# Norm weights on the sync queue, matmul order pinned between sublayers, and twelve weight units per feed-forward part in tiles of the attention

## The chip, the cores and the metric

The kernel runs on one core of a Trainium2 chip. The metric is the device time of one execution in microseconds (us). A profiled execution also has a span, from its first to its last instruction; the time is a little longer than the span.

## The reference

Four layers work on x of 256 rows and 1024 columns, in float32. Each layer is an attention sublayer and then a feed-forward sublayer, and each sublayer is wrapped in two norms:

```
for i in range(4):
    hn = rms_norm(x, norm_gains[i, 0])
    m  = mixer[i % 3](hn)             # a: differential attention, b: stick-breaking, c: sliding window with sinks
    x  = x + rms_norm(m, norm_gains[i, 1])
    f  = (silu(h @ w_gate) * (h @ w_up)) @ w_down,  h = rms_norm(x, norm_gains[i, 2])
    x  = x + rms_norm(f, norm_gains[i, 3])
```

The hidden width is 2816. Layers 0 and 3 use mixer a, layer 1 mixer b, layer 2 mixer c. Mixers a and c rotate queries and keys by position (rope).

## The kernel before

**Streams and units.** The 256 rows are two streams, s=0 and s=1, of 128 rows each. All weights are cut into 378 units of 128x1024 numbers. A unit is fetched by the sync queue (SP) into one of STAGE=4 tiles `stage`. ScalarE (ACT) then rounds it into `hi`, and VectorE (DVE) writes the remainder `lo` (function `split`, L254). Both live in a ring of RING=11 tiles each. Stream 0 uses a unit first, stream 1 some units later; the ring slot is free when stream 1 is done with it. With 512 columns a stream spends six matmuls of 512 columns on a unit: hi and lo by the rounded activations (`xh`), and hi by their remainder (`xl`), each twice.

**The order of emission.** `Emitter` (L42) is a planner that runs while the program is built. Each stream is a generator; it asks for a unit, waits for an event, or sleeps for some planned nanoseconds (`yield ("d", 4000)`). Shorter generators, its tasks, turn tiles and compute scores. The planner's clock `t` moves forward with every emitted matmul. Stream 0 goes first unless stream 1 is behind an edge (the start of an output projection, or the end of a layer). Stream 0 may lead by at most LAG=8 units, and units are split at most AHEAD=3 beyond stream 0 and RING=11 beyond stream 1:

```
while self.loaded < min((self.pos[0] + AHEAD if self.pos[0] else 2), free, self.limit):
...
return self.pos[s] in self.ring and (lag < (LAG if self.pos[1] > 3 else 3) if s == 0 else lag > 0)
```

**The order on the engines.** The framework's scheduler may reorder what was emitted: it fills each engine's list with the instruction of the best rank that its own model believes ready. The list is then fixed, and an engine works through it in order. An instruction wrapped in `tc.keep_in_program_order` comes behind everything emitted before it on its engine; later ones that are not wrapped may still be moved ahead of it. The class `Start` (L172) wraps the calls of an engine while its flag `on` is set. `act.on`, `dve.on` and `pool.on` are cleared in layer 0 when stream 1's first norm is emitted, `pe.on` after stream 1's first projected chunk (L516).

**Around the change.** Between two sublayers a stream runs `post_norm` (squares on ACT, `r` on GpSimd (POOL), `mg` and the new `x` on DVE), sleeps 4000, runs `pre_norm` (eight transposes `tp_q` or `tp_n` of `x` on TensorE (PE), `xh` on ACT, `xl` on DVE), sleeps 600 and asks for its first unit. In the feed-forward part, chunk c takes four units of gate and up weights, and from c=1 on two units of down weights (`down`, results `acc_f`) follow. The hidden values `h_f` go through POOL (`hp_f`), a transposing DMA and POOL again (`hx_f`) before ACT and DVE split them into `hTh_f` and `hTl_f`. In mixer c, task `keys` (L806) ropes the first chunk on DVE into `kd_c`, then transposes it on PE (`tk_c`). In mixer a, task `turned` (L604) ropes a chunk into `t_a...` on DVE and then transposes it (`tt_a...`).

**The start.** `rows`, the norm weights as 128x128, and `pos_i`, the positions, are fetched on ACT's queue in that order (L276, L278). On SP's queue come x of stream 0, two units, x of stream 1 and two more units. `tables()` (L317) works on DVE from the positions, and the copy `gains` of the turned norm weights follows it there; `xh_n` needs `gains`.

**Tiles of the attention.** Keys and values have a tile for each group g and stream s (`kT{g}{s}`, `V{g}{s}`), attention weights one for each stream (`wT{s}`). Once stream 1's attention output is turned, nothing reads them until the next layer.

Of the kernel before, what the change touches and what calls it, by code (L numbers as in the profile page):

```python
# [9 lines left out]
F32 = mybir.dt.float32  # L10
# [31 lines left out]
class Emitter:  # L42
# [3 lines left out]

    def __init__(self, load_dma, split, n_units, edges):
        self.t = 0.0  # L50
        self.load_dma, self.split, self.n, self.edges = load_dma, split, n_units, edges
        self.issued = self.loaded = 0
        self.pos = [0, 0]
        self.ring = {}
        self.events = set()
        self.limit = 0
        self.tasks = []
# [10 lines left out]
            self.issued += 1  # L68

    def advance(self):  # L70
        free = self.pos[1] + RING
        while self.loaded < min((self.pos[0] + AHEAD if self.pos[0] else 2), free, self.limit):
            self.fetch(self.loaded + STAGE)
            self.ring[self.loaded] = self.split(self.loaded)
            self.loaded += 1

    def run_task(self, task):
        while True:
# [34 lines left out]
    def can(self, m):  # L113
        if m["done"]:
            return False
        if m["want"] is None:
            return True
        if m["want"] == "w":
            s = m["s"]
            lag = self.pos[0] - self.pos[1]  # L120
            return self.pos[s] in self.ring and (lag < (LAG if self.pos[1] > 3 else 3) if s == 0 else lag > 0)
        return m["want"] in self.events

    def run(self, gens):
# [34 lines left out]
def trunk_kernel(ctx, tc, x, positions, norm_gains, a_w_in, a_w_out, a_lambda, a_subln, b_w_in, b_w_out,  # L159
# [12 lines left out]
    class Start:  # L172


        def __init__(self, engine):
            self.engine, self.on = engine, True
# [37 lines left out]
    def downs(c):  # L214

        return range(c - 1, c) if 0 < c < NCH - 2 else range(NCH - 3, NCH) if c == NCH - 1 else ()

    for i in range(depth):
        kind, inst = i % 3, i // 3
        if kind in (0, 1):  # L220
            w_in, w_out = (a_w_in[inst], a_w_out[inst]) if kind == 0 else (b_w_in[inst], b_w_out[inst])
            for g in range(2):
                for part in range(3):
                    chunk512(w_in, part * 1024 + 512 * g)
        else:
            w_in, w_out = c_w_in[inst], c_w_out[inst]
            chunk256(w_in, 1024)
            for g in range(4):
                chunk256(w_in, 256 * g)
        edges.append(len(units))  # L230
        for kt in range(KT):
            rows_unit(w_out, kt)
        for c in range(NCH):
            gate_up(i, c)
            for d in downs(c):
                for j in range(2):
                    rows_unit(w_down[i], 2 * d + j)
        edges.append(len(units))

    staged = {}  # L240
# [12 lines left out]

    def split(u):  # L254
        t = staged.pop(u)
        hi = ringp.tile([P, 1024], F32R, tag="hi", name=f"hi_{u}")
        lo = ringp.tile([P, 1024], F32R, tag="lo", name=f"lo_{u}")
        act.activation(hi, t, AF.Copy)
        dve.tensor_tensor(lo, t, hi.bitcast(F32), ALU.subtract)
        return hi, lo  # L260

    em = Emitter(load_dma, split, len(units), edges)


    zero = wk.tile([P, P], BF16, tag="t2k", name="zero", bufs=TMP)
# [7 lines left out]
    warming(WARM // 2)  # L273

    rows = wk.tile([P, P], F32, tag="t2k", name="rows", bufs=TMP)
    nc.scalar.dma_start(rows, norm_gains.rearrange("l n (k p) -> (l n k) p", p=P))  # L276
    pos_i = wk.tile([2, P], I32, tag="t2k", name="pos_i", bufs=TMP)
    nc.scalar.dma_start(pos_i, positions.rearrange("b (s p) -> (b s) p", p=P))  # L278
    xs = [cst.tile([P, D], F32, name=f"x_{s}") for s in range(2)]
# [222 lines left out]
    def project(s, xn, n, units_, name, first, tag="mm"):  # L502

        b = bank("acc" if first else tag, s, [P, n], f"mm_{name}")
        per = KT // units_
        for u in range(units_):
            w = yield ("w",)
            js = [(per * u + j, slice(j * n, (j + 1) * n)) for j in range(per)]
            pairs = [(kt, cs, v) for kt, cs in js for v in range(2)]
            if pe.on:  # L510
                pairs.sort(key=lambda x: x[2])
            for kt, cs, v in pairs:
                mm(b, xn[0][:, kt, :], w[v][:, cs], kt == 0 and v == 0, False)
            for kt, cs in js:
                mm(b, xn[1][:, kt, :], w[0][:, cs], False, kt == KT - 1)
        if s:  # L516
            pe.on = False
        return b

    def rope(b, n, cr, sr, name, outs=None):  # L520
# [28 lines left out]
        act.activation(dst, tp, AF.Copy)  # L549

    kT, V = {}, {}

    def queries(s, n, name):
        return wk.tile([P, n, P], F32, tag=f"qT{s}", name=f"qT_{name}", bufs=1)
# [41 lines left out]
    def layer_a(s, i, xn):  # L596
# [7 lines left out]
        def turned(chunk, g, which):  # L604
            t = rope(chunk, 8, *tabs[which], f"{name}{g}{which}")
            yield ("d", 2000)
            dst = None
            if which == "k":
                dst = kT[g, s] = wk.tile([P, 4, P], F32, tag=f"kT{g}{s}", name=f"kT_{name}{g}", bufs=1)
            else:  # L610
                dst = qT[g] = queries(s, 4, f"{name}{g}")
            four_transposes(s, t.rearrange("p h d -> p (h d)"), dst, f"tt_{name}{g}{which}")
            em.set((name, which, g))
            if which == "k":
                yield from scores(g)
# [73 lines left out]
        for g in range(2):  # L689
            for which in "qkv":  # L690
                chunk = yield from project(s, xn, 512, 4, f"{name}{g}{which}", g == 0 and which == "q")
                if not tabs:
                    tabs.update(scaled_tables(s, xn[2], name))
                if which == "v":
                    V[g, s] = wk.tile([P, 512], F32, tag=f"V{g}{s}", name=f"V_{name}{g}", bufs=1)
                    act.activation(V[g, s], chunk, AF.Copy, scale=xn[2])
                    em.set((name, "v", g))
                    em.spawn(values(g))
                    yield ("d", 600)
                else:  # L700
                    em.spawn(turned(chunk, g, which))
                    yield ("d", 1500)
        return oT, name

    def layer_b(s, i, xn):
# [6 lines left out]
        def turned(chunk, g, which):  # L712
            t = wk.tile([P, 512], F32, tag="t2k", name=f"t_{name}{g}{which}", bufs=TMP)
            act.activation(t, chunk, AF.Copy, scale=xn[2])
            yield ("d", 900)
            dst = None
            if which == "k":
                dst = kT[g, s] = wk.tile([P, 4, P], F32, tag=f"kT{g}{s}", name=f"kT_{name}{g}", bufs=1)
            else:
                dst = qT[g] = queries(s, 4, f"{name}{g}")  # L720
            four_transposes(s, t, dst, f"tt_{name}{g}{which}")
            em.set((name, which, g))
            if which == "k":
                yield from scores(g)
# [60 lines left out]
        for g in range(2):  # L785
            for which in "qkv":
                chunk = yield from project(s, xn, 512, 4, f"{name}{g}{which}", g == 0 and which == "q")
                if which == "v":
                    V[g, s] = wk.tile([P, 512], F32, tag=f"V{g}{s}", name=f"V_{name}{g}", bufs=1)
                    act.activation(V[g, s], chunk, AF.Copy, scale=xn[2])  # L790
                    em.set((name, "v", g))
                    em.spawn(values(g))
                    yield ("d", 600)
                else:
                    em.spawn(turned(chunk, g, which))
                    yield ("d", 600)
        return oT, name

    def layer_c(s, i, xn):
# [6 lines left out]
        def keys(chunk):  # L806
            kd = wk.tile([P, 2, 2, 64], F32, tag="t2k", name=f"kd_{name}", bufs=TMP)
            rope(chunk[:, 0:P], 2, *tabs["k"], f"{name}k", [kd[:, :, 0, :], kd[:, :, 1, :]])
            V["c", s] = wk.tile([P, P], F32, tag=f"V0{s}", name=f"V_{name}", bufs=1)
            act.activation(V["c", s], chunk[:, P:2 * P], AF.Copy, scale=xn[2])  # L810
            yield ("d", 1200)
            tp = bank("tp", s, [P, 2, P], f"tk_{name}")
            for c in range(2):
                transpose(tp[:, c, :], kd[:, c].rearrange("p a d -> p (a d)"))
            t = kT["c", s] = wk.tile([P, 2, P], F32, tag=f"kT0{s}", name=f"kT_{name}", bufs=1)
            act.activation(t, tp, AF.Copy)
            em.set((name, "k"))

# [117 lines left out]
    def stream(s):  # L936
        if s:
            yield ("d", 1500)
        for i in range(depth):
            kind = i % 3  # L940
            xn = pre_norm(s, 4 * i, f"n{i}{s}")
            yield ("d", 600)
            if i == 0 and s:
                em.spawn(scalars())
            oT, name = yield from (layer_a, layer_b, layer_c)[kind](s, i, xn)
            gain = gain_of(i, 1)
            acc = yield from out_proj(s, oT, name, (1, 1, 3)[kind])
            post_norm(s, acc, gain, f"m{i}{s}")
            yield ("d", 4000)
            gain = gain_of(i, 3)  # L950
            xn = pre_norm(s, 4 * i + 2, f"q{i}{s}")
            yield ("d", 600)
            acc = yield from ffn(s, i, xn)
            post_norm(s, acc, gain, f"e{i}{s}")
            if i < depth - 1:
                yield ("d", 4000)
        for h in range(2):
            cs = slice(h * 512, (h + 1) * 512)
# [28 lines left out]
```

## Time and profile before

| | |
|---|---|
| median of three runs | 1187.56 us (1186.59 to 1187.84) |
| profiled execution | 1186.93 us, span 1185.1 us |
| granted TensorE clock | 0.998 |
| busy: PE, DVE, ACT, POOL | 1162.8, 784.8, 654.4, 216.9 us |
| instructions | 16743 |

In timeline rows the columns are start, duration, engine, line, operation, out<-in, count, and in brackets the idle time of the engine before it with what ended it. Nearly all rows name L182, since the class `Start` issues most instructions from there; they are told apart by tile names. Rows that end in q (SPq, ACTq) are issues of DMAs. The end of a matmul is modelled, so losses on PE are best read from one start to the next.

### The profile page before, as it was taken

The page shows a single profiled execution, that of the slowest core. Times are in us where ns is not written, and L with a number is a line of the kernel's source. Part 1 is how long each engine was busy: PE and PEld are TensorE (multiplying, and loading weights), DVE is VectorE, ACT ScalarE, POOL GpSimd, SP SyncE. Part 2 cuts the span into 40 slices and gives each one's busy share as a digit, 9 for nine tenths or more (in the row PEclk, how much of TensorE's full clock was granted, in tenths as well). Part 3 has the DMA queues.
Part 4 walks back from the last instruction along what each step waited for, and adds up shares of the span by engine and source line. Part 5 has one row for each costly group of instructions (what it writes and reads, how often), then busy time and mean ns, then how long its engine had stood idle before and what let it go on. Part 6 is the DMA issues. An engine that isn't in the chain of part 4 may idle for free.

```text
span 1185.1 us, 16743 instructions
## 1 busy us (share of the span) xinstructions
PE 1162.8 (98%) x5869; PEld 954.8 (81%) x5869; DVE 784.8 (66%) x1226; ACT 654.4 (55%) x1209; POOL 216.9 (18%) x301
## 2 busy tenths in 40 slices
PE   8999999999999999999999999999999999999997
PEld 6787788888878878888888878888878788888886
DVE  7876666665847666666588666666686775766563
ACT  6665654444766655445476655444475565544441
POOL 2100133221200013222210013222210001322221
PEclk9999999999999999999999999999999999999999
DMA  7635468777643646777664346777765364687761
GB/s 265 208 126 177 129 195 231 202 220 207 216 128 125 213 129 196 206 217 212 203 195 154 108 129 196 215 212 216 207 195 155 130 192 150 178 211 213 209 194 40
DMA packets 183948, 216.41 MB, mean 183 GB/s; under 512 B 52788, under 2 KB 148152, under 8 KB 183864
## 3 DMA queue, kind: packets, MB, share of 16 engines
q1 hardware_dynamic: 183716, 215.28, 60.9%
q8 instruction: 46, 0.75, 0.2%
q14 instruction: 38, 0.31, 0.1%
q10 hardware_dynamic: 148, 0.07, 0.0%
HBM read 203.76 MB, written 1.05 MB: 173 GB/s over the span
## 4 chain that ended last, share of the span: by engine, by line
PE 90%; DVE 3%; ACT 2%; issue 2%; DMA 1%; POOL 1%; DVEq 0%; ACTq 0%; POOLq 0%; SPq 0%
PE mm_f L182 39%; PE acc_f L182 19%; PE acc_a L182 3%; PE mm_c L182 2%; PE acc_b L182 2%; PE sc_a L182 2%; PE acc_c L182 2%; DVE lo L182 1%; ACT hi L182 1%; PE sc_c L182 1%; PE sc_b L182 1%; DMA stage<-in_a_w_in_dram 1%; PE pv_a L182 1%; DVE x L182 1%; PE tp_q L182 1%
## 5 line engine op out<-in xcount | busy, mean ns | idle before, releaser
L182 DVE TENSOR_TENSOR lo<-stage,hi 128x1024 fp32r<-128x1024 f32 x378 | 459.5, 1225 | 160.0 <-ACT hi L182 157.8
L182 ACT ACTIVATE hi<-stage 128x1024 fp32r<-128x1024 f32 x378 | 395.1, 1057 | 166.2 <-PE mm_f L182 85.7
L182 PE MATMUL mm_f<-hi,xh_q 128*128 128x512 f32 x704 | 275.4, 391 | 1.5 <-ACT hi L182 1.5
L182 PE MATMUL mm_f<-lo,xh_q 128*128 128x512 f32 x704 | 274.0, 389 | 0.0
L182 PE MATMUL mm_f<-hi,xl_q 128*128 128x512 f32 x704 | 217.0, 389 | 0.4 <-DVE xl_q L182 0.4
L182 POOL COPY hp_f<-h_f 128x512 uint16<-128x512 uint16 x80 | 92.0, 1149 | 408.2 <-DVE h_f L182 408.2
L182 PEld LDWEIGHTS mm_f<-hi,xh_q 128*128 128x128 f32 x704 | 132.1, 188 | 30.3 <-ACT hi L182 3.2
L182 PEld LDWEIGHTS mm_f<-hi,xl_q 128*128 128x128 f32 x704 | 132.1, 188 | 28.9 <-DVE xl_q L182 1.3
L182 PEld LDWEIGHTS mm_f<-lo,xh_q 128*128 128x128 f32 x704 | 132.2, 188 | 27.0
L182 ACT ACTIVATE hTh_f<-hx_f 128x256 fp32r<-128x256 f32 x80 | 33.4, 418 | 163.4 <-POOL hx_f L182 163.4
L182 PE MATMUL acc_f<-hi,hTh_f 128*128 128x512 f32 x352 | 111.4, 392 | 1.2 <-ACT hTh_f L182 1.2
L182 PE MATMUL acc_f<-lo,hTh_f 128*128 128x512 f32 x352 | 109.8, 389 | 0.0
L182 PE MATMUL acc_f<-hi,hTl_f 128*128 128x512 f32 x352 | 109.8, 389 | 0.0
L182 DVE TENSOR_TENSOR hTl_f<-hx_f,hTh_f 128x256 fp32r<-128x256 f32 x80 | 33.8, 423 | 103.5 <-ACT hTh_f L182 103.5
L182 POOL COPY hx_f<-hq_f 128x512 uint16<-128x512 uint16 x80 | 80.5, 1006 | 84.1 <-DMA hq_f<-hp_f 83.8
L182 ACT ACTIVATE t_f<-mm_f,half_f 128x256 f32<-128x256 f32 x88 | 41.5, 472 | 77.4 <-PE mm_f L182 77.4
L182 PEld LDWEIGHTS acc_f<-hi,hTh_f 128*128 128x128 f32 x352 | 65.8, 188 | 15.5 <-ACT hTh_f L182 2.4
L182 PEld LDWEIGHTS acc_f<-lo,hTh_f 128*128 128x128 f32 x352 | 66.1, 188 | 13.8
L182 PEld LDWEIGHTS acc_f<-hi,hTl_f 128*128 128x128 f32 x352 | 66.0, 188 | 13.7
L182 DVE SCALAR_TENSOR_TENSOR t_f<-t_f,mm_f 128x256 f32<-128x256 f32 x88 | 36.7, 417 | 34.3 <-ACT t_f L182 34.3
L182 DVE SCALAR_TENSOR_TENSOR h_f<-t_f,hsq_f,mm_f 128x256 f32<-128x256 f32 x88 | 42.2, 480 | 2.9
L182 ACT ACTIVATE e_a<-sc_a,nm_a 128x128 f32<-128x128 f32 (+1 forms) x64 | 26.1, 421 | 16.5 <-DVE nm_a L182 16.4
(588 smaller groups left out, 1545.5 us busy)
## 6 DMA issues: line engine op xcount, KB each, us to landing
stage<-in_ffn_w_gate_dram SPq DMA_DIRECT2D x176, 256.0 KB, 3.0
stage<-in_ffn_w_up_dram SPq DMA_DIRECT2D x176, 256.0 KB, 3.2
stage<-in_ffn_w_down_dram SPq DMA_DIRECT2D x88, 512.0 KB, 4.4
stage<-in_a_w_in_dram SPq DMA_DIRECT2D x48, 512.0 KB, 4.2
stage<-in_b_w_in_dram SPq DMA_DIRECT2D x24, 512.0 KB, 4.1
stage<-in_a_w_out_dram SPq DMA_DIRECT2D x16, 512.0 KB, 3.7
stage<-in_c_w_in_dram SPq DMA_DIRECT2D x10, 512.0 KB, 4.0
gain<-in_norm_gains_dram SPq DMA_DIRECT2D x8, 512.0 KB, 5.1
```

What stands on the lines that cost most here:

```text
L182: i = call(*args, **kw)
```

## The change

1. `rows` is fetched first on SP's queue, ahead of x; `pos_i` is then alone on ACT's queue.
2. `hold` keeps a count that starts at 2. Every `post_norm` that another sublayer follows adds one, and every stream's first unit of a sublayer, after its matmuls, takes one away; `pe.on` is set while the count is above 0. So PE's instructions are pinned to the order of emission while a stream is between sublayers. At the start this ends after each stream's first unit, earlier than before. The sort of pairs in `project` now goes by `act.on`.
3. The sleep behind `pre_norm` is 1100 in place of 600, other than ahead of layer 0.
4. Each feed-forward part has 66 units. Twelve of them (k = 2, 5, 8, 16, 19, 22, 30, 33, 36, 44, 47, 50) are split into the tiles `kT0`/`V0`, `kT1`/`V1` or `wT1` in place of ring slots, once stream 1's attention output is turned (event `("a01", "o", 7)` and the like). `lead` lets stream 0 be ahead by LAG plus the number of such units from 11 behind it to 2 beyond, so by up to 11.
5. For this the two groups' keys share a tile for each stream, and so do the values.

```
+        self.before, last, ring = [], {}, 0
+        for u, home in enumerate(homes):
+            slot = home[0] if home else ring % RING
+            ring += not home
+            self.before.append(last.get(slot, -1))
+            last[slot] = u
...
     def advance(self):
-        free = self.pos[1] + RING
-        while self.loaded < min((self.pos[0] + AHEAD if self.pos[0] else 2), free, self.limit):
+        while self.loaded < min((self.pos[0] + AHEAD if self.pos[0] else 2), self.limit):
+            home = self.homes[self.loaded]
+            if self.before[self.loaded] >= self.pos[1] or home and home[1] not in self.events:
+                break
...
+    def lead(self):
+        u = self.pos[0]
+        return LAG + sum(home is not None for home in self.homes[max(u - RING, 0):u + AHEAD])
...
-            return self.pos[s] in self.ring and (lag < (LAG if self.pos[1] > 3 else 3) if s == 0 else lag > 0)
+            return self.pos[s] in self.ring and (lag < (self.lead() if self.pos[1] > 3 else 3) if s == 0 else lag > 0)
...
+    holds = 2
+    def hold(n):
+        nonlocal holds
+        holds += n
+        pe.on = holds > 0
...
+    def free_places(i, n):
+        done = ("abc"[i % 3] + f"{i}1", "o", 7)
+        places = {2: "first", 5: "second", 8: "weights"}
+        homes.extend((places[k % 14], done) if k % 14 in places and k < n - 14 else None for k in range(n))
...
-        hi = ringp.tile([P, 1024], F32R, tag="hi", name=f"hi_{u}")
-        lo = ringp.tile([P, 1024], F32R, tag="lo", name=f"lo_{u}")
+        if homes[u] is None:
+            hi, lo = (ringp.tile([P, 1024], F32R, tag=p, name=f"{p}_{u}") for p in ("hi", "lo"))
+        elif homes[u][0] == "weights":
+            both = wk.tile([P, 2, 1024], F32R, tag="wT1", name=f"hl_{u}", bufs=1)
+            hi, lo = both[:, 0, :], both[:, 1, :]
+        else:
+            n = 0 if homes[u][0] == "first" else 1
+            hi, lo = (wk.tile([P, 1024], F32R, tag=f"{p}{n}", name=f"{q}_{u}", bufs=1) for p, q in (("kT", "hi"), ("V", "lo")))
...
-    nc.scalar.dma_start(rows, norm_gains.rearrange("l n (k p) -> (l n k) p", p=P))
+    tc.keep_in_program_order(nc.sync.dma_start(rows, norm_gains.rearrange("l n (k p) -> (l n k) p", p=P)))
...
-            if pe.on:
+            if act.on:
                 pairs.sort(key=lambda x: x[2])
...
-        if s:
-            pe.on = False
+            if first and u == 0:
+                hold(-1)
...
-            yield ("d", 600)
+            yield ("d", 1100 if i else 600)
...
             post_norm(s, acc, gain, f"m{i}{s}")
+            hold(1)
             yield ("d", 4000)
             gain = gain_of(i, 3)
             xn = pre_norm(s, 4 * i + 2, f"q{i}{s}")
-            yield ("d", 600)
+            yield ("d", 1100)
             acc = yield from ffn(s, i, xn)
             post_norm(s, acc, gain, f"e{i}{s}")
             if i < depth - 1:
+                hold(1)
                 yield ("d", 4000)
```

More of the change, by code (lines that the diff above doesn't have):

```diff
@@ L42, with __init__ @@
 class Emitter:
-    def __init__(self, load_dma, split, n_units, edges):
+    def __init__(self, load_dma, split, n_units, edges, homes):
         self.t = 0.0
         self.load_dma, self.split, self.n, self.edges = load_dma, split, n_units, edges
+        self.homes = homes
+        self.before, last, ring = [], {}, 0
[4 more added lines that the diff above has]
+            last[slot] = u
         self.issued = self.loaded = 0
@@ L187, in trunk_kernel @@
     act, dve, pool, pe = (Start(e) for e in (nc.scalar, nc.vector, nc.gpsimd, nc.tensor))
+    holds = 2
[3 more added lines that the diff above has]
+        pe.on = holds > 0
     units, edges = [], []
+    homes = []
     def cols_unit(w, kt0, n_kt, c0, n):
@@ L232, in trunk_kernel @@
             rows_unit(w_out, kt)
+        homes.extend([None] * (len(units) - len(homes)))
         for c in range(NCH):
@@ L237, in trunk_kernel @@
                     rows_unit(w_down[i], 2 * d + j)
+        free_places(i, len(units) - len(homes))
         edges.append(len(units))
@@ L260, in split @@
         return hi, lo
-    em = Emitter(load_dma, split, len(units), edges)
+    em = Emitter(load_dma, split, len(units), edges, homes)
     zero = wk.tile([P, P], BF16, tag="t2k", name="zero", bufs=TMP)
@@ L551, in trunk_kernel, with keys_of, values_of @@
     kT, V = {}, {}
+    def keys_of(g, s, name):
+        if g == 0:
+            both = wk.tile([P, 2, 4, P], F32, tag=f"kT{s}", name=f"kT_{name}", bufs=1)
+            for n in range(2):
+                kT[n, s] = both[:, n]
+        return kT[g, s]
+    def values_of(g, s, name):
+        if g == 0:
+            both = wk.tile([P, 2, 512], F32, tag=f"V{s}", name=f"V_{name}", bufs=1)
+            for n in range(2):
+                V[n, s] = both[:, n]
     def queries(s, n, name):
@@ L608, in turned @@
             if which == "k":
-                dst = kT[g, s] = wk.tile([P, 4, P], F32, tag=f"kT{g}{s}", name=f"kT_{name}{g}", bufs=1)
+                dst = keys_of(g, s, name)
             else:
@@ L694, in layer_a @@
                 if which == "v":
-                    V[g, s] = wk.tile([P, 512], F32, tag=f"V{g}{s}", name=f"V_{name}{g}", bufs=1)
+                    values_of(g, s, name)
                     act.activation(V[g, s], chunk, AF.Copy, scale=xn[2])
@@ L717, in turned @@
             if which == "k":
-                dst = kT[g, s] = wk.tile([P, 4, P], F32, tag=f"kT{g}{s}", name=f"kT_{name}{g}", bufs=1)
+                dst = keys_of(g, s, name)
             else:
@@ L788, in layer_b @@
                 if which == "v":
-                    V[g, s] = wk.tile([P, 512], F32, tag=f"V{g}{s}", name=f"V_{name}{g}", bufs=1)
+                    values_of(g, s, name)
                     act.activation(V[g, s], chunk, AF.Copy, scale=xn[2])
@@ L808, in keys @@
             rope(chunk[:, 0:P], 2, *tabs["k"], f"{name}k", [kd[:, :, 0, :], kd[:, :, 1, :]])
-            V["c", s] = wk.tile([P, P], F32, tag=f"V0{s}", name=f"V_{name}", bufs=1)
+            V["c", s] = wk.tile([P, P], F32, tag=f"V{s}", name=f"V_{name}", bufs=1)
             act.activation(V["c", s], chunk[:, P:2 * P], AF.Copy, scale=xn[2])
@@ L814, in keys @@
                 transpose(tp[:, c, :], kd[:, c].rearrange("p a d -> p (a d)"))
-            t = kT["c", s] = wk.tile([P, 2, P], F32, tag=f"kT0{s}", name=f"kT_{name}", bufs=1)
+            t = kT["c", s] = wk.tile([P, 2, P], F32, tag=f"kT{s}", name=f"kT_{name}", bufs=1)
             act.activation(t, tp, AF.Copy)
```

## The prediction

> **What bounds the kernel now.** I read the page first: busy time, clock and the chain that ended last.
>
> ```profile
> span 1185.1 us, 16743 instructions
> ...
> PE 1162.8 (98%) x5869; PEld 954.8 (81%) x5869; DVE 784.8 (66%) x1226; ACT 654.4 (55%) x1209; POOL 216.9 (18%) x301
> ...
> PE 90%; DVE 3%; ACT 2%; issue 2%; DMA 1%; POOL 1%; DVEq 0%; ACTq 0%; POOLq 0%; SPq 0%
> ...
> L182 ACT ACTIVATE hi<-stage 128x1024 fp32r<-128x1024 f32 x378 | 395.1, 1057 | 166.2 <-PE mm_f L182 85.7
> ```
>
> TensorE (PE) is busy 98% of the span and is 90% of the chain. The change removes no matmul, so all it can win is PE's idle time, 1185.1 - 1162.8 = 22 us (1.9%), less what the first norm and the last output must cost. The last row says that `hi` waits 85.7 us for matmuls of the feed-forward part: for ring slots, as stream 1 is their last reader. Next I asked by windows where PE idles: one in mid feed-forward, then the four places where stream 1 goes from attention to feed-forward.
>
> ```profile
> core 0: us, PE busy (x), PEclk, DMA share, GB/s
> 200.00:205.00 5.00, 5.00 (x23) 1.00 0.70 215
> 141.00:146.00 5.00, 3.98 (x20) 1.00 0.36 108
> 440.00:445.00 5.00, 3.98 (x20) 1.00 0.32 102
> 706.00:711.00 5.00, 3.48 (x19) 1.00 0.27 91
> 1006.00:1011.00 5.00, 3.97 (x20) 1.00 0.27 92
> ```
>
> Mid feed-forward PE has no hole at full clock, so more buffers win nothing there. The four crossings have the same hole. The timeline of the first, all engines:
>
> ```profile
> 141.22 1.05 ACT L182 ACTIVATE hi<-stage 128x1024 fp32r<-128x1024 f32 x1
> 141.34 0.61 PE L182 MATMUL mm_f<-hi,xl_q 128*128 128x512 f32 x2
> 141.78 0.76 POOL L182 COPY hx_f<-hq_f 128x512 uint16<-128x512 uint16 x1
> 142.32 0.49 PE L182 MATMUL mm_f<-hi,xh_q 128*128 128x512 f32 x1 [0.37 <-ACT hi L182]
> 143.04 0.50 PE L182 MATMUL acc_f<-hi,hTh_f 128*128 128x512 f32 x1 [0.23 <-ACT hTh_f L182]
> 143.08 1.41 DVE L182 SCALAR_TENSOR_TENSOR x<-mg_m,r_m,x 128x512 f32<-128x512 f32 x2 [1.03 <-POOL r_m L182]
> 143.98 0.63 PE L182 MATMUL tp_q<-ident,x 128*128 128x128 f32 x4 [0.43 <-DVE x L182]
> 145.06 0.50 PE L182 MATMUL mm_f<-hi,xh_q 128*128 128x512 f32 x1
> 146.60 0.60 DVE L182 SCALAR_TENSOR_TENSOR xl_q<-tp_q,gains,xh_q 128x128 fp32r<-128x128 f32 x2
> ```
>
> A 512-column matmul takes 0.227 us from start to start when nothing waits (23 of them in the 5.00 us of mid feed-forward are 22 intervals). So the two at 141.34 end at 141.80. From there PE waits for `hi` (to 142.32: 0.52), after one matmul for `hTh` (142.55 to 143.04: 0.49), after another for `x` (143.27 to 143.98: 0.71): 1.72 us a crossing, 6.9 us in four.
>
> **The change part by part.**
>
> *The start.*
>
> ```profile
> 0.72 0.41 ACTq L276 DMA_DIRECT2D rows<-in_norm_gains_dram  x1
> 0.72 0.39 SPq L280 DMA_DIRECT2D x<-in_x_dram  x1
> 1.16 0.54 ACTq L278 DMA_DIRECT2D pos_i<-in_positions_dram  x1
> 5.21 0.22 DVE L182 CAST pos_f<-pos_i 2x128 f32<-2x128 int32 x1 [4.29 <-DMA pos_i<-in_positions_dram]
> 6.54 1.06 ACT L182 ACTIVATE hi<-stage 128x1024 fp32r<-128x1024 f32 x1 [3.30 <-DMA stage<-in_a_w_in_dram]
> 9.00 0.28 DVE L182 COPY gains<-tp_gain 128x128 f32<-128x128 f32 x1
> 9.38 1.14 ACT L182 ACTIVATE xh_n<-tp_n,gains 128x128 fp32r<-128x128 f32 x4 [1.78 <-DVE gains L182]
> out_dram<-x SPq DMA_DIRECT2D x4, 256.0 KB, 2.0
> ```
>
> The positions land 4.0 us after their issue (1.16 to 5.2), and the table work on DVE, `gains` and `xh_n` follow them without slack. Moved, `pos_i` issues at 0.72: at least 0.44 us won. x and the first units issue some 0.41 us later behind `rows`; ACT's first `hi` then ends at 6.54 + 0.41 + 1.06 = 8.0, and `xh_n` behind it on ACT can start at 8.04 in place of 9.38: at most 1.34 won. A landing of 3.1 us would reach that; the nearest row for a transfer with little ahead of it is 2.0 us, so I take 1.2. SP's other early issues move by the same 0.41 and are covered while `hi` waits behind `gains`.
>
> [...]
>
> *Twelve units in the attention's tiles.* Mid feed-forward: nothing, as the window is full. At a crossing it counts what stream 0 still has ready. Before, stream 0 stood 8 ahead when stream 1 took its last output-projection unit: one ready unit (six matmuls, 1.36 us), then down units that wait for `hTh`, and a gate-up unit whose `hi` had to wait for the slot of the very unit stream 1 had just finished, behind two squares on ACT. After, it stands 11 ahead: the next unit and the two behind it are gate-up units of chunk 2, in slots freed earlier. That is 18 x 0.227 = 4.1 us of ready work; stream 1's `x` takes 143.98 - 140.44 = 3.5 us (the unit ahead of the hole starts six matmuls, 1.36 us, before 141.80). So the first two waits go. The third need not: PE's list is fixed when built, and before, it put the transposes behind one unit and two matmuls though `x` came 0.71 us later still, after two other waits. If they stand as early again, PE waits the whole 1.7 for `x`; if they stand well, nothing. I take the middle, 0.85 won each, 3.4 in four. Bounds: 0 and 6.9. If stream 1's attention output is turned late, the third unit splits late: a wait for one `hi` (1.06) and its `lo`, taken as 0, since ACT and DVE have idle time there.
>
> *Order kept.* Where PE's list already follows the emission this changes nothing. It differs in four places of the feed-forward to attention crossings of layers 2 and 3:
>
> ```profile
> 610.85 0.62 PE L182 MATMUL acc_f<-lo,hTh_f 128*128 128x512 f32 x2
> 612.03 0.39 PE L182 MATMUL mm_c<-hi,xh_n 128*128 128x256 f32 x1 [0.55 <-ACT xh_n L182]
> ...
> 613.99 0.39 PE L182 MATMUL acc_f<-hi,hTl_f 128*128 128x512 f32 x1
> ...
> 614.93 0.64 PE L182 MATMUL mm_c<-hi,xl_n 128*128 128x256 f32 x4
> 615.41 0.28 PE L182 MATMUL mm_c<-hi,xh_n 128*128 128x256 f32 x1
> ...
> 617.10 1.42 DVE L182 SCALAR_TENSOR_TENSOR x<-mg_e,r_e,x 128x512 f32<-128x512 f32 x2 [0.36 <-POOL r_e L182]
> 619.96 0.49 DVE L182 TENSOR_TENSOR kd_c<-t_c20k 128x128 f32<-128x128 f32 x2
> 620.72 0.38 PE L182 MATMUL tk_c<-ident,kd_c 128*128 128x128 f32 x2
> 876.63 0.62 PE L182 MATMUL acc_f<-lo,hTh_f 128*128 128x512 f32 x2
> 878.08 0.50 PE L182 MATMUL mm_a300q<-hi,xh_n 128*128 128x512 f32 x1 [0.82 <-ACT xh_n L182]
> 885.47 1.03 PE L182 MATMUL tp_n<-ident,x 128*128 128x128 f32 x8
> 888.01 0.68 DVE L182 TENSOR_TENSOR t_a300q<-t_a300q 128x512 f32<-128x512 f32 x1
> 888.86 0.60 PE L182 MATMUL tt_a300q<-ident,t_a300q 128*128 128x128 f32 x4
> ```
>
> (a) In both layers stream 0's first projection was moved ahead of stream 1's last down units and waited for `xh_n`: 612.03 - 611.30 = 0.7 and 878.08 - 877.08 = 1.0. Pinned behind them it finds `xh_n` ready: 1.7 won.
>
> (b) Layer 2. Stream 1's `post_norm` sleeps 4000, in which stream 0 emits two units of planned 1280 each and `keys`, asleep for 1200, its transposes: 3760, so `tk_c` now stands right behind 24 short matmuls and ahead of stream 1's `tp_n`. They end at about 616.1 on this clock: the last down matmul ends at 613.99 + 0.23, less 0.7 of (a) and the two `mm_c` hoisted there, plus 24 x 0.12 (614.93 to 615.41 is four). `kd_c` was done at 620.45. Nothing later can fill in: stream 1 has no `xh_n` yet, and stream 0's next chunks are pinned behind. If DVE keeps its order (x, rope, a `lo`, rope) PE waits 4.3 us; if rope goes ahead of x, in DVE's idle time from 617.10 - 0.36 on (0.49 for `kd_c` and about as much for the two products), 1.5. Before, PE worked on chunk 1 there. I take 3.0.
>
> (c) Layer 3. Four units fill more than 4000, so `tp_n` comes as before; then one unit (1.36) and `tt_a300q`, pinned, where before a second unit came first. PE arrives at 885.47 + 0.8 (the eight transposes) + 1.36 = 887.6; rope ends at 888.69. A loss of 0 to 1.1; I take 0.8.
>
> In layer 1, and in all four crossings of stream 0 into the feed-forward part, PE's list already follows the emission: 0. A pin that a crossing of stream 1 adds stands ahead of `tp_q` and of stream 1's first unit; what is emitted behind these isn't pinned and may still be moved ahead, which is why the 4.1 us of work can serve as cover.
>
> *The rest.* Sleeps of 1100: the other stream's unit was emitted in that place already, 0. Sorting by `act.on` and pins that end earlier in layer 0: a few 0.227 us matmuls change places, 0 within 0.6 either way. Shared key and value tiles: same bytes, same readers, 0.
>
> *Sum.* -1.2 - 3.4 - 1.7 + 3.0 + 0.8 = -2.5 us against the profiled execution's 1186.93: 1184.4. It is 0.63 below the median of the three runs, so against that 1187.56 - 2.5 = 1185.1, 0.2% faster (2.4 us is 0.2%, about what a measurement of this kernel tells from no change).
>
> **Rivals.**
>
> R1, the hole goes wholly: the ready units stand where they are needed, crossings lose nothing: -1.2 - 6.9 - 1.7 + 3.8 = -6.0, 1181.6. For it: the waits for `hi` and `hTh` go for sure, and 4.1 us of work exceed 3.5 us of latency. Against it: the 0.71 us by which the list ran ahead of `x`. [...]
>
> R2, slower: the pins hold the cover back. If PE's list has `tp_q` directly behind the single pinned unit and stream 1's first unit directly behind that, a crossing loses 143.98 - 141.80 = 2.2 us for `x`, and after four matmuls (0.9 from 145.06) another 0.9 until the first `xl_q` is there at 146.9: 3.1 in place of 1.72. Sum -1.2 + 5.5 - 1.7 + 3.8 = +6.4, 1194.0. It decides once a crossing loses over 2.1 us: 1.72 + (2.4 - 0.9)/4. For it: everything in that stretch is pinned. Against: units behind it aren't.
>
> R3, no change: the extra lead is used up before the crossing and the list puts `tp_q` as early as before; crossings still lose 1.72: -1.2 - 1.7 + 3.8 = +0.9, 1188.5.
>
> **How the numbers follow.** The forecast gets 0.4, R1 0.2, R2 0.17, R3 0.23. The forecast's 2.5 us stand just past 2.4, so its 0.4 divides about evenly (0.22 faster, 0.18 same); R1 is faster; R3 is mostly same, a little slower; R2 is slower. Together 0.43, 0.37, 0.20. With all bounds on the good side (-1.3 - 6.9 - 1.7 + 1.5) it is 1179.2; with the bad ones of the start and of (b) and (c) and no gain at crossings (-0.4 - 1.7 + 5.4), 1190.9. I give 1179.5 to 1190.0, which leaves out most of R2.
>
> **What would show it.** Start: `pos_f` before 4.5, the first `mm_a000q` near 8.5, not 9.80. Crossings: no wait of `mm_f` for `hi`; `tp_q` behind two or three units of `mm_f`, with a wait for `x` under 1 us. Layers 2 and 3: no `mm_c` or `mm_a300q` amid the last `acc_f`; a hole of 1.5 to 4.3 us ahead of `tk_c`, one below 1.1 ahead of `tt_a300q`. Wrong it would be made by another order of DVE's list around `kd_c`, by scheduling differences inside the attention parts (their scattered waits are 0.2 to 1.2 us each), or by crossings that still have one unit of cover.

## The result, and the profile after

The changed kernel takes 1197.28 us (median of 4 runs, 1196.06 to 1197.75) against 1187.4 for the kernel before beside it: ratio 1.0081, 95% interval 1.0069 to 1.0093. It is slower by 9.9 us; I had forecast 1185.1. The profiled execution took 1196.06 us. From the page of the changed kernel (line 196 is now the line that records every operation):

```profile
span 1194.3 us, 16856 instructions
...
PE 1166.4 (98%) x5869; PEld 956.6 (80%) x5869; DVE 786.7 (66%) x1226; ACT 657.2 (55%) x1209; POOL 223.8 (19%) x301
...
PE 84%; DVE 5%; ACT 3%; issue 3%; DMA 2%; POOL 2%; SPq 0%; DVEq 0%; POOLq 0%; ACTq 0%
```

PE's share of the chain fell from 90% to 84%, DVE's rose from 3% to 5%: PE waits more often for a vector result. The waits of PE in the changed kernel (total us, times, longest):

```profile
PE to_a L196 <- DVE on_a L196: 3.2, 3, 1.4
PE acc_f L196 <- DVE x L196: 3.1, 1, 3.1
PE tp_q L196 <- DVE x L196: 3.1, 3, 1.0
PE tk_c L196 <- DVE kd_c L196: 2.7, 1, 2.7
PE tt_a300q L196 <- DVE t_a300q L196: 1.3, 1, 1.3
PE acc_f L196 <- DVE hTl_f L196: 1.1, 2, 0.8
PE ta_b L196 <- ACT aT_b L196: 1.0, 1, 1.0
```

Of these, `tk_c`, `tt_a300q` and `ta_b` are not in the same list of the kernel before, and `acc_f` had four waits of at most 0.5. To see where the time moves along the kernel, I subtracted the start times of the same matmul in the two timelines; between two marks stand the same matmuls (but for 0.4 us of them that e7 and e12 move from att. 3 to FFN 3), so a row shows how much idle or slow time PE gained. In the table "attention" is the move from a layer's first `tp_n` (layer 0: from the start) to stream 0's first `tp_q`, and "FFN" from there to the next layer's first `tp_n`, so that it holds the end of stream 1's attention, its crossing and the feed-forward part. Each row is against the kernel before; the experiments come below. The lists of e4 are the changed kernel's on every engine, so these two rows are one program run twice, and an entry can move by 0.7 between two runs.

| us against before | att. 0 | FFN 0 | att. 1 | FFN 1 | att. 2 | FFN 2 | att. 3 | FFN 3 | span |
|---|---|---|---|---|---|---|---|---|---|
| changed kernel | -2.18 | +0.11 | +1.24 | -0.24 | +4.01 | +3.79 | +1.21 | +1.19 | +9.13 |
| e1 no kept order | -1.69 | +0.11 | +0.98 | -0.23 | +0.20 | -0.78 | +0.03 | +1.07 | -0.31 |
| e2 no units | -2.40 | +0.03 | +1.01 | +0.04 | +4.15 | +0.59 | +0.58 | +0.05 | +4.04 |
| e3 rows alone | -1.11 | +0.04 | +0.54 | +0.03 | +0.07 | +0.01 | -0.02 | 0.00 | -0.43 |
| e4 short sleeps | -1.98 | +0.15 | +1.27 | -0.16 | +3.99 | +3.85 | +0.55 | +1.13 | +8.80 |
| e5 kept into attention | -2.16 | +0.06 | +1.94 | -0.22 | +5.43 | +0.05 | +1.43 | +1.07 | +7.60 |
| e6 kept into FFN | -2.10 | +0.14 | +1.85 | -0.16 | +0.15 | +4.16 | -0.10 | +1.12 | +5.05 |
| e7 late turns | -1.91 | +0.09 | +2.34 | -0.21 | +2.35 | +2.81 | +1.24 | +1.17 | +7.87 |
| e9 early turn | -2.36 | +0.08 | +2.22 | -0.17 | +4.01 | -0.20 | +1.73 | +1.13 | +6.43 |
| e10 units in layer 2 | -1.74 | +0.01 | +0.19 | +0.04 | +0.04 | -0.79 | +0.02 | -0.02 | -2.25 |
| e12 both mends | -2.21 | +0.09 | +1.45 | -0.18 | +2.36 | -0.20 | +0.96 | +1.32 | +3.59 |

The change loses in layer 2 above all: 4.0 us in its attention part and 3.8 where I had expected a gain. The places one by one. The start, all engines:

```profile
0.72 0.53 ACTq L315 DMA_DIRECT2D pos_i<-in_positions_dram  x1
2.10 0.23 DVE L196 CAST pos_f<-pos_i 2x128 f32<-2x128 int32 x1 [1.19 <-DMA pos_i<-in_positions_dram]
6.40 1.06 ACT L196 ACTIVATE hi<-stage 128x1024 fp32r<-128x1024 f32 x1 [3.62 <-DMA stage<-in_a_w_in_dram]
7.77 0.50 PE L196 MATMUL mm_a000q<-hi,xh_n 128*128 128x512 f32 x1 [0.96 <-ACT xh_n L196]
```

`pos_f` comes at 2.10 (5.21 before), the first `mm_a000q` at 7.77 (9.80): the start wins 2.0. The first crossing of stream 1, PE alone:

```profile
142.90 0.39 PE L196 MATMUL mm_f<-hi,xh_q 128*128 128x512 f32 x1
...
144.94 0.39 PE L196 MATMUL mm_f<-lo,xh_q 128*128 128x512 f32 x1
146.37 0.66 PE L196 MATMUL tp_q<-ident,x 128*128 128x128 f32 x4 [1.03 <-DVE x L196]
```

Ten `mm_f` run from 142.90 without a wait, then PE waits for `x` alone: 146.37 - 144.94 - 0.23 = 1.20 us, where before it lost 1.72 in three waits. (This is time over the pitch, the 0.227 us from one such matmul to the next; the idle time in brackets, 1.03, is less, since the end of a matmul is modelled.) Layers 1 and 3 look the same. So these crossings gain 0.5 each, but the attention's end ahead of them pays. DVE there (layer 0):

```profile
116.83 3.54 DVE L196 TENSOR_TENSOR lo<-stage,hi 128x1024 fp32r<-128x1024 f32 x3
120.28 0.16 DVE L196 SCALAR_TENSOR_TENSOR os_a<-os_a,el_a 128x4 f32<-128x4 f32 x1
...
122.48 0.69 DVE L196 TENSOR_TENSOR on_a<-pv_a,os_a 128x512 f32<-128x512 f32 x1 [0.90 <-POOL os_a L196]
```

Three `lo` stand in DVE's list ahead of `os_a` (3.54 us), where there were two before, and `to_a` on PE waits 0.95 for `on_a` behind it, where it did not wait before; in layer 3 it waits 1.45. In layer 1 it is ACT: `aT_b` stands behind a `hi` that waits for its weights.

```profile
412.18 1.06 ACT L196 ACTIVATE hi<-stage 128x1024 fp32r<-128x1024 f32 x1 [4.73 <-DMA stage<-in_ffn_w_up_dram]
413.15 0.58 ACT L196 ACTIVATE aT_b<-ta_b 128x512 f32<-128x512 f32 x1
```

The starts of layers 2 and 3 (PE):

```profile
615.56 0.64 PE L196 MATMUL mm_c<-hi,xl_n 128*128 128x256 f32 x4
618.88 0.44 PE L196 MATMUL tk_c<-ident,kd_c 128*128 128x128 f32 x2 [2.68 <-DVE kd_c L196]
...
895.62 0.65 PE L196 MATMUL tt_a300q<-ident,t_a300q 128*128 128x128 f32 x4 [1.27 <-DVE t_a300q L196]
```

Both transposes stand where I had put them, and lose 2.84 and 1.43 us over the pitch. Last, stream 1's crossing in layer 2, first PE, then GpSimd and SP's queue, then what the profile says of the tile `hTh_f` there:

```profile
709.16 0.39 PE L196 MATMUL acc_c<-hi,ol_c 128*128 128x512 f32 x1
712.70 1.88 PE L196 MATMUL acc_f<-hl,hTh_f 128*128 128x512 f32 x4 [3.15 <-DVE x L196]
...
717.13 0.39 PE L196 MATMUL mm_f<-hi,xh_q 128*128 128x512 f32 x1
...
718.50 1.04 PE L196 MATMUL tp_q<-ident,x 128*128 128x128 f32 x8
```

```profile
701.65 0.61 POOL L196 COPY hp_f<-h_f 128x512 uint16<-128x512 uint16 x1 [9.38 <-DVE h_f L196]
710.54 0.30 POOL L196 TENSOR_SCALAR u_m<-ssp_m 128x1 f32<-128x1 f32 x1 [8.28 <-ACT junk_m L196]
710.92 0.57 POOL L196 TENSOR_TENSOR r_m<-u_m,mhalf 128x1 f32<-128x1 f32 x1
711.44 0.75 POOL L196 COPY hx_f<-hq_f 128x512 uint16<-128x512 uint16 x1
```

```profile
702.28 1.21 SPq L626 DMA_TRANSPOSE hq_f<-hp_f  x1
```

```profile
L196 ACT ACTIVATE hTh_f<-hx_f x1: 416/416/416, 712.2 to 712.2; 128x256 fp32r<-128x256 f32 x1
...
  ACT hTh_f L196: 3.6, 1
```

In the kernel before, PE went from one ready unit and one more matmul to `tp_q` here, with 0.53 us lost for `hi` and 1.43 for `x`:

```profile
706.46 0.49 PE L182 MATMUL mm_f<-hi,xh_q 128*128 128x512 f32 x1 [0.37 <-ACT hi L182]
708.11 0.63 PE L182 MATMUL tp_q<-ident,x 128*128 128x128 f32 x4 [1.16 <-DVE x L182]
```

In the changed kernel stream 1's last output unit ends at 709.39. Next in PE's list stand twelve `acc_f`, two down units of stream 0, and they need `hTh_f`. Its transposing DMA was issued at 702.28, but the copy `hx_f` stands behind `u_m` and `r_m` of stream 1's norm on GpSimd, which sat idle for 8.28 us until stream 1's last unit was through. So `hTh_f` ends at 712.65 and PE goes on at 712.70, 3.3 us late. (The row names `x`, whose first half ends at the same moment; the weight load of these matmuls waited 3.6 us for `hTh_f` by the last fence.) The twelve matmuls then take 717.13 - 712.70 = 4.43 us where 12 x 0.227 = 2.73 were due. The windows of PE show why (columns: stretch, length, busy, granted clock, DMA share, GB/s):

```profile
616.00:618.80 2.80, 0.20 (x2) 1.00 0.07 26
618.80:623.00 4.20, 4.12 (x35) 1.00 0.47 165
...
712.70:714.00 1.30, 1.30 (x4) 0.59 0.00 0
714.00:715.00 1.00, 1.00 (x4) 0.50 0.61 125
...
716.00:717.00 1.00, 1.00 (x5) 0.82 0.47 168
```

After the 3.15 us of waiting the clock is 0.50 from 714 to 716, 0.82 from 716 to 717 and 1.00 from 717 to 718; after the 2.68 ahead of `tk_c` it stayed at 1.00.

### The profile page after: what moved, and what is told of

It is laid out like the page before. It is cut to its first block, busy times and chain, and to the rows that moved or that the text cites. A ratio compares the mean times of both kernels' runs of the same rounds, so it can differ in the third digit from the quotient of the medians.

```text
span 1194.3 us, 16856 instructions
## 1 busy us (share of the span) xinstructions
PE 1166.4 (98%) x5869; PEld 956.6 (80%) x5869; DVE 786.7 (66%) x1226; ACT 657.2 (55%) x1209; POOL 223.8 (19%) x301
## 4 chain that ended last, share of the span: by engine, by line
PE 84%; DVE 5%; ACT 3%; issue 3%; DMA 2%; POOL 2%; SPq 0%; DVEq 0%; POOLq 0%; ACTq 0%
PE mm_f L196 39%; PE acc_f L196 18%; DVE lo L196 2%; PE acc_a L196 2%; PE mm_c L196 2%; PE sc_a L196 2%; ACT hi L196 1%; DMA stage<-in_a_w_in_dram 1%; PE acc_c L196 1%; PE acc_b L196 1%; PE sc_c L196 1%; DMA stage<-in_ffn_w_up_dram 1%; POOL os_a L196 1%; PE pv_c L196 1%; PE sc_b L196 1%
## 5 line engine op out<-in xcount | busy, mean ns | idle before, releaser
L196 DVE TENSOR_TENSOR lo<-stage,hi 128x1024 fp32r<-128x1024 f32 x362 | 440.2, 1226 | 166.8 <-ACT hi L196 159.9
L196 ACT ACTIVATE hi<-stage 128x1024 fp32r<-128x1024 f32 x362 | 379.9, 1059 | 175.5 <-PE mm_f L196 34.8
L196 PE MATMUL mm_f<-hi,xh_q 128*128 128x512 f32 x672 | 262.6, 391 | 0.0
L196 PE MATMUL mm_f<-lo,xh_q 128*128 128x512 f32 x672 | 261.7, 389 | 0.0
L196 PE MATMUL mm_f<-hi,xl_q 128*128 128x512 f32 x672 | 208.1, 390 | 0.5 <-DVE xl_q L196 0.5
L196 POOL COPY hx_f<-hq_f 128x512 uint16<-128x512 uint16 x80 | 89.7, 1123 | 112.4 <-DMA hq_f<-hp_f 111.8
L196 PE MATMUL acc_f<-hi,hTh_f 128*128 128x512 f32 x320 | 100.7, 392 | 0.5 <-ACT hTh_f L196 0.5
L196 PE MATMUL acc_f<-hi,hTl_f 128*128 128x512 f32 x320 | 100.1, 390 | 1.1 <-DVE hTl_f L196 1.1
L196 PE MATMUL acc_f<-lo,hTh_f 128*128 128x512 f32 x320 | 100.0, 390 | 0.0
L196 POOL TENSOR_TENSOR os_a<-os_a,mhalf 128x4 f32<-128x4 f32 x8 | 9.9, 1243 | 142.2 <-DVE os_a L196 142.2
```

The source lines that it names most:

```text
L196: i = call(*args, **kw)
```

## The experiments

**Which part costs?** Four kernels with one part undone or alone.

e1, without the kept order:

```
             post_norm(s, acc, gain, f"m{i}{s}")
-            hold(1)
...
             if i < depth - 1:
-                hold(1)
```

> The changed kernel with neither `hold(1)`: PE is pinned at the start alone, everything else of the change stays. Theory P (the pinned order makes the loss): the holes ahead of `tk_c` (2.8 us), `tt_a300q` (1.4) and `acc_f` in layer 2 (3.3, and 1.8 of slower matmuls behind it) go, the two early first projections of layers 2 and 3 come back (+1.7); the start keeps its 2.2: 1197.3 - 9.3 + 1.7 = 1189.7, or less. Theory U (the longer lead makes it): the holes of the feed-forward crossings and of `to_a` and `ta_b` stay, and only those of `tk_c` and `tt_a300q` go: 1197.3 - 4.2 + 1.7 = 1194.8.

1186.78 us (0.9995 of before, 0.9987 to 1.0004), as P said. The kept order is the whole loss, some 10.5 us. Without it the `tk_c`, `tt_a300q` and 3.3 us `acc_f` waits are gone; the waits of `to_a` and `ta_b` and the 1.2 us of `tp_q` stay, so they do not come from the kept order.

e2, without the units in dead tiles (the lead is 8 again):

```
-        homes.extend((places[k % 14], done) if k % 14 in places and k < n - 14 else None for k in range(n))
+        homes.extend([None] * n)
```

> The changed kernel with all units in the ring (no unit in a tile of the attention, lead 8 as before); pins, sleeps and the start stay. Theory P: the holes of layers 2 and 3 ahead of `tk_c` and `tt_a300q` stay (4.2), and the crossings into the feed-forward part lose at least the old 1.7 each, more if `tp_q` is pinned behind one unit: 1194 to 1200. Theory U: down units no longer stand ahead of stream 1's norm, so the 5.1 us of layer 2's crossing and the holes of `to_a` and `ta_b` (3.9) go: 1197.3 - 9 + 2 = 1190.

1191.08 us (1.0032, 1.0021 to 1.0043): P's range is missed, and U's 1190 is 1.1 off. `to_a` waits 0.8 once, as before, and `ta_b` not at all, so their waits belong to the units; the 2.7 us for `kd_c` stay, as P said. The kept order alone costs some 5 us against e3, nearly all ahead of and in layer 2's attention (+4.15); its crossing loses 0.6, not 3.8. So layer 2's crossing needs both parts.

e3, the kernel before with the norm weights on the sync queue alone:

```
-    nc.scalar.dma_start(rows, ...)
+    tc.keep_in_program_order(nc.sync.dma_start(rows, ...))
```

> The kernel before with one edit: `rows` first on the sync queue. If the start's gain belongs to this edit alone, the first `mm_a000q` starts near 7.6 us as in the changed kernel (9.80 before) and 1.2 to 2.2 us are kept to the end: 1185.2 to 1186.2. If the pins that end earlier in layer 0 made part of it, or other waits give it back, 1187.

1186.19 us (0.9991, 0.9982 to 1.0), 1.3 us less and just within what can be measured. The first `mm_a000q` starts at 8.10, 1.7 earlier than before but not at 7.6, and the matmuls behind it come 0.43 us apart, about twice the pitch, until past 10.5. In its span 1.11 is left of the gain when layer 0's attention ends, and 0.54 is given back at the start of layer 1.

e4, the planner's sleeps back at 600:

```
-            yield ("d", 1100 if i else 600)
+            yield ("d", 600)
...
-            yield ("d", 1100)
+            yield ("d", 600)
```

> The changed kernel with the sleep behind `pre_norm` at 600 as before; all else stays. Theories P and U: no effect of the sleep by itself, within 1 us of 1197.3. Rival S (the longer sleep moves stream 1's units and the attention's transposes against each other and makes the holes of `to_a`, `ta_b` and the later first unit): 1193.

1197.74 us (1.0084, 1.007 to 1.0097): no effect, since no engine's list changes.

**Two places or one chain of consequences?** e5 keeps the order into the attention parts only, e6 into the feed-forward parts only.

```
 e5:  post_norm(s, acc, gain, f"m{i}{s}")
-     hold(1)
 e6:  if i < depth - 1:
-         hold(1)
 both:
-     holds += n
+     holds = max(holds + n, 0)
```

> The changed kernel with the emission order kept only from a feed-forward part into the next attention (the hold after the attention's post_norm is left out); rows, homes, lead, sleeps as in the change. Theory P2 (the kept order costs in two separate places: some 4 us ahead of and in the attention parts of layers 1 to 3, and some 5 us at layer 2's crossing into the feed-forward part, the latter only together with the units in dead tiles): the 3.3 us wait of acc_f for hTh_f at about 709 us goes, the waits of tk_c for kd_c (2.8) and of tt_a300q (1.4) stay; 1186.8 without any hold plus 4.4 gives 1191.2 (1190.0 to 1192.5). Rival Q (the layer 2 crossing is bad because the attention before it was put late by the kept order, one chain of consequences): the 3.3 us wait stays, 1195 or more. Rival Z (the cost sits all in the crossings into the feed-forward part): 1188 or less.

1193.31 us (1.0054, 1.0041 to 1.0066), 0.8 above P2's range. The crossing of layer 2 is clean (+0.05), so Q and Z fall; but layer 2's attention costs 5.4 here, 1.4 more than in the changed kernel. The windows of PE show where: behind the same wait for `kd_c` (2.67 us, up to 619.56) the granted clock is 0.50 from 621 to 622, where it stayed at 1.00 in the changed kernel, and the matmuls from 620 to 624 lose 1.5 us.

```profile
621.00:622.00 1.00, 1.00 (x6) 0.50 0.95 385
```

> The changed kernel with the emission order kept only from an attention part into the feed-forward part (the hold at the end of the feed-forward part is left out). Theory P2: tk_c and tt_a300q no longer wait, mm_c and mm_a300q are drawn ahead of stream 1's last units again (waits of 0.7 to 1.0 for xh_n come back), the 3.3 us wait of acc_f for hTh_f in layer 2 and the low clock behind it stay: 1186.8 plus 5 gives 1191.8 (1190.5 to 1193.0). Rival Q (that wait hangs on the kept order at the start of layer 2): 1188 or less. Rival Z: 1196 or more.

1190.99 us (1.0031, 1.002 to 1.0043), as P2 said. The attention parts cost nothing more than in e1, bar layer 1's start, and layer 2's crossing the same as in the changed kernel. PE there:

```profile
708.80 1.65 PE L196 MATMUL acc_f<-hl,hTh_f 128*128 128x512 f32 x3 [3.15 <-DVE x L196]
```

**The attention starts.** e7 keeps everything and tells the planner a longer way to the transposes:

```
 keys:           yield ("d", 1200)  ->  yield ("d", 4500)
 layer_a turned: yield ("d", 2000)  ->  yield ("d", 4000 if i else 2000)
```

> The whole change, with the planner told of a longer way from a projection to its transpose: 4500 in place of 1200 ahead of tk_c, 4000 in place of 2000 ahead of the tt_a transposes of layer 3. If the waits of tk_c and tt_a300q come from transposes that the planner emits before VectorE can have made their operand, and that then stand there because their order is kept, both fall below 0.5 us, and the time falls by the two waits, 2.84 and 1.43, to 1193.0 (1192.0 to 1194.5). Rival: something else is late there (the norm's reciprocal, the tables of cosines) and another matmul waits in the place of tk_c: the holes stay within 1 us of what they were, 1196 to 1198.

1194.79 us (1.0062, 1.0049 to 1.0074), 2.5 us less. Both waits are gone:

```profile
617.74 1.29 PE L196 MATMUL tp_n<-ident,x 128*128 128x128 f32 x8 [0.16 <-DVE x L196]
...
621.74 0.38 PE L196 MATMUL tk_c<-ident,kd_c 128*128 128x128 f32 x2
```

But 2.84 + 1.43 = 4.3 us of waits bought only 2.5: later in layer 2 `mm_c` now loses 1.7 waiting for a rope, and in layer 3 `mm_a301k` and `mm_a311k` lose 0.7 and 0.9. So it just misses its range.

**Layer 2's crossing.** e8 keeps the units but gives stream 0 the old lead:

```
-        return LAG + sum(...)
+        return LAG
```

> The whole change, but the lead of stream 0 in units is LAG everywhere, also while units lie in dead tiles; the twelve homes stay. Theory L (the longer lead lets stream 0 run ten units and then stream 1 its last three output units in a row, so that down units whose hx_f stands behind stream 1's norm on GpSimd are pinned ahead of tp_q): the 3.3 us wait of acc_f at layer 2's crossing falls under 1 us, the waits of tk_c and tt_a300q stay, 1192 (1190.5 to 1193.5), as without homes. Rival H (the homes alone make it, by the changed lists of ScalarE and VectorE): the wait stays, 1196 to 1198.

1230.91 us (1.0367, 1.0353 to 1.0382): both theories miss. The feed-forward parts of the four layers now lose 7 to 11 us each. The wait lists of the sync queue and of ACT show what is late (total us, times, longest):

```profile
SPq L626 <- POOL hp_f L196: 306.7, 46, 13.4
ACT hi L196 <- DMA stage<-in_ffn_w_down_dram: 164.9, 42, 8.6
```

The sync queue stands for 306.7 us at transposing DMAs that wait for `hp_f` (142.6 in the changed kernel), the weights whose fetch stands behind them are late, and `hi` waits 164.9 us for down weights where it waited 1.0. Why the plain lead brings about this order stays open. The 3.3 us wait left layer 2, as L said, and waits of 3.36, 3.35 and 2.75 us came up at the three other crossings, each time with an `acc_f` ahead of `tp_q` that starts 0.05 us after `hTh_f` ends: the pattern is not special to layer 2.

e9 alters one number, and with it every engine's list at layer 2's crossing alone:

```
-            yield ("d", 4200)
+            yield ("d", 2500 if i == 2 and s == 0 and c == 0 else 4200)
```

> The whole change with one number altered: in layer 2 the planner is told that chunk 0 of stream 0's feed-forward part is turned after 2500 in place of 4200, so that its copy on GpSimd, its hTh_f and hTl_f, and its two down units are emitted ahead of stream 1's norm and not behind it; elsewhere every engine's list is the same. Theory B (that chain stood behind stream 1's norm in the lists of GpSimd, ScalarE and VectorE, although its transposing DMA had landed long before, and the kept order of TensorE put the waiting matmuls ahead of tp_q): the 3.3 us wait goes, and with it the 1.7 us lost to the lower clock behind it; at the crossing a wait of tp_q for x of about 1.2 stays, as at the other three: 1197.3 less 3.3 and 1.7, plus 1.2, gives 1193.5 (1192.0 to 1194.5). Rival N (the norm of stream 1 is itself late there, so that whatever stands in that place waits): a wait of 2.5 us or more stays, 1196 to 1198.

1193.81 us (1.0051, 1.0037 to 1.0065), 3.5 less, as B said. GpSimd and PE at that crossing:

```profile
705.67 0.77 POOL L196 COPY hx_f<-hq_f 128x512 uint16<-128x512 uint16 x1 [2.57 <-DMA hq_f<-hp_f]
...
713.90 0.30 POOL L196 TENSOR_SCALAR u_m<-ssp_m 128x1 f32<-128x1 f32 x1 [4.93 <-ACT junk_m L196]
```

```profile
714.95 0.39 PE L196 MATMUL mm_f<-lo,xh_q 128*128 128x512 f32 x1
716.37 0.66 PE L196 MATMUL tp_q<-ident,x 128*128 128x128 f32 x4 [1.03 <-DVE x L196]
```

`hx_f` now runs as soon as its DMA lands, the down units go between stream 1's output units, and the crossing is like the other three: FFN 2 moves from +3.79 to -0.20.

e12 makes both mends, e7's and e9's:

> The whole change with both mends: the longer way to the transposes of layers 2 and 3 that the planner is told (4500 and 4000), and the early turn of chunk 0 in layer 2. If the two causes are separate, the gains add: 1194.8 less what the early turn gains (3.8) gives 1191.0 (1190.0 to 1192.0); what is then left over the run without kept order, some 4 us, is the kept order's other cost, in the attention parts themselves. Rival (the mended attention moves layer 2's crossing, and the wait appears in another place): 1193 or more.

1190.86 us (1.0029, 1.0017 to 1.004), as reckoned: the two causes add. The 4.1 us left over e1 lie mostly in the attention parts, 2.2 of them in layer 2's by the table.

**The units.** e10 drops the kept order and places units in dead tiles in layer 2 alone:

```
-        free_places(i, len(units) - len(homes))
+        if i == 2:
+            free_places(i, len(units) - len(homes))
+        else:
+            homes.extend([None] * (len(units) - len(homes)))
```

> The change without the kept order, and with the units in dead tiles in layer 2 alone (in the other layers every unit is in the ring, and the lead follows). Reckoned from the run without kept order against the kernel before, whose span moved by +0.1, +0.8, -0.8 and +1.1 us over the attention ends and crossings of layers 0 to 3: the units lose in layers 1 and 3, where the first transposes behind the attention wait for VectorE, and gain in layer 2. If these add up one by one: 1186.8 less 0.1, 0.8 and 1.1 gives 1184.9 (1184.2 to 1185.8). Rival (each layer's loss is an accident of the order that the layers before it leave, so that layer 2 changes as well): 1186.0 to 1187.5.

1183.97 us (0.9972, 0.9961 to 0.9982): faster than the kernel before and than every other kernel here; 0.2 below the range. PE at layer 2's crossing (the last output unit starts its last matmul at 703.91):

```profile
707.47 1.21 PE L196 MATMUL acc_f<-hl,hTh_f 128*128 128x512 f32 x4 [0.44 <-ACT hTh_f L196]
708.51 0.60 PE L196 MATMUL tp_q<-ident,x 128*128 128x128 f32 x4
```

The same down units stand at the same place, but with their order free the scheduler put two units of `mm_f` ahead of them, which cover the norm, and set `tp_q` among the `acc_f`. Before, 1.95 us were lost in this crossing over the pitch; now 0.6 ahead of `acc_f` and 0.7 at the first `xl_q`.

e11, also without the kept order, keeps one unit of three in dead tiles:

```
-        places = {2: "first", 5: "second", 8: "weights"}
+        places = {5: "second"}
```

> The change without the kept order, with four units in dead tiles in place of twelve: one for each feed-forward part (the sixth unit, in the places of kT1 and V1). Theory W (the waits of to_a and ta_b at the ends of the attention parts come from three splits of units in a row, which ScalarE and VectorE then have ahead of the last head's work): these waits (1.1, 1.0 to 1.2, 1.5 to 1.6 us) fall to 0.5 or less, the wait of tp_q for x lies between 1.2 and the 1.7 of before, and the time is 1185.5 to 1186.5. Rival V (any unit split ahead of the attention's end does it): the waits stay, 1186.8 to 1187.8.

1215.52 us (1.0234, 1.022 to 1.0248): it cannot tell W and V apart, as the feed-forward parts again lose 6 to 8 us each. What it and e8 share is a lead of 8 or 9 with units that wait for a fixed tile. The sync queue waits 241.4 us for `hp_f` here, more than in the changed kernel and less than in e8, but `hi` waits only 2.5 for down weights and 30.7 for up weights; the cause stays open.

## Why the prediction was wrong

The steps, in its order.

- *Start, -1.2.* Right in kind, too small: 2.2 by layer 0's attention in the changed kernel, 1.1 with the rows alone. The cap that I had set, ACT's first `hi` at 6.95 and `xh_n` behind it at 8.04, was too late: they started at 6.40 and 7.37. I had taken 2.0 us as the nearest landing; `pos_i` took 2.10 - 0.72 = 1.4. With `rows` ahead of it on its queue `pos_i` needed 4.0 us, with `rows` on the other queue 1.4.
- *Units, -3.4 at four crossings.* Three crossings went as described, with the waits for `hi` and `hTh` gone and a wait of 1.20 for `x`, so 0.5 won each where I had taken 0.85, the middle of 0 and 1.7. I had allowed, at 0, for units that split late behind a late attention output; it is the output that comes late behind the splits of the units, and `to_a` and `ta_b` wait 1.0 to 1.6 for it. e1 and e2 put that on the units: in layers 1 and 3 they lose more than they gain. By the spans e1, which has units and start but no kept order, is 0.1 us above e3, the start alone: the units won nothing. Nor was the hole the same at all four: layer 2's was 1.95, as the windows row with 3.48 us busy already hinted.
- *(a), -1.7.* `mm_c` and `mm_a300q` do stand behind stream 1's down units now, but there `acc_f` waits 0.98 and 0.43 for `hTl_f`: nothing in layer 2, half a microsecond in layer 3.
- *(b), +3.0, and (c), +0.8.* Both waits came, at 2.84 and 1.43. What I left out is behind them: layer 2's attention loses some 1.7 more than (a) and (b) say, and mending the two waits (e7) leaves about 2.4 of the 4.0.
- *"In layer 1, and in all four crossings of stream 0 into the feed-forward part, PE's list already follows the emission: 0", and the sentence behind it on stream 1.* **This is the step that failed.** I asked only what is emitted behind `tp_q` and might move ahead. I did not ask what is emitted ahead of it. With the longer lead these are in layer 2 two down units of stream 0 whose chain stands behind stream 1's norm on GpSimd, and which are now pinned there. With a free order the scheduler puts ready work ahead of them (as in e10). Cost: FFN 2 at +3.79 where e1 has -0.78, 4.6 us; the wait (3.3) and the slow matmuls at the lower clock (1.7), less a wait of 0.6 that e1 has of its own there, make 4.4 of it.

Sum: forecast -2.5, span +9.1. The 11.6 between them are -1.0 at the start, 4.6 in FFN 2 (from -0.85), 1.7 in layer 2's attention (from +2.3), 1.4 in layer 3's (from -0.2), and 4.9 over the other three crossings with their attention ends (from -0.85 each). Taken by parts, I had +2.1 for the kept order, and by the spans of the changed kernel and e1 it cost 9.4. R2 had the sign and the cause (pins hold the cover back) but the wrong place: `tp_q` stood behind ten matmuls or more at every crossing, never behind one unit. Layer 1's start is a sum of its own: where it is +1.5 or more, as in e9, ACT's third `hi` waits for its weights, with the same lists as in the changed kernel:

```profile
317.34 1.06 ACT L196 ACTIVATE hi<-stage 128x1024 fp32r<-128x1024 f32 x1 [1.41 <-DMA stage<-in_b_w_in_dram]
```

That is the transfer's landing in that execution, and part of what the earlier start gives back.

## What to carry to other kernels

Before an order is pinned, list for each pinned instruction when its operand is ready by the trace, and on which engine's list the operand's maker stands behind what; a scheduler that moves ready work ahead hides errors of the plan that a pin lays bare. More buffers change the lists of the engines that fill them too: look at what the fills are put ahead of. And try a change's parts by themselves and layer by layer: the new start with a quarter of the units, and no pins, won 3.5 us where the whole lost 9.9.

## What was not expected of the hardware

In these traces TensorE's granted clock is down to 0.50 after some waits of 2.7 to 3.4 us (0.55 in the mean after one of 2.28) and stays at 1.00 after others of 2.7 to 3.4. The wait for `kd_c` shows both: 2.68 us in the changed kernel with the clock at 1.00 behind it, 2.67 in e5 with 0.50. In e8 PE had waited 3.36 and 3.35 us ahead of 144.7 and 455.7, again with opposite outcomes:

```profile
144.50:148.80 4.30, 4.08 (x22) 1.00 0.00 0
...
455.60:460.00 4.40, 4.29 (x17) 0.68 0.02 6
...
887.20:891.00 3.80, 3.63 (x8) 0.55 0.28 71
```

Ahead of the last row the wait was 2.28 us, and the clock fell all the same, as the matmul at its start in e8's timeline shows:

```profile
887.33 1.22 PE L196 MATMUL acc_f<-hi,hTh_f 128*128 128x512 f32 x2 [2.28 <-ACT hi L196]
```

In the changed kernel the clock is at 0.50 for 3 us (713 to 716) and 1.00 again from 716.5. By these runs a wait of this length costs its own time and, in some places and not in others, more behind it: 1.7 us after the 3.15 us wait of the changed kernel.
